# Attention's value products in two passes over a stationary tile that holds both halves of V, with the softmax denominators summed on GpSimd

## The chip, the cores and the metric

The kernel runs on one core of one Trainium2 chip. The metric is the time of one launch in microseconds (us) of device time. The engines are named as the profile names them: PE (TensorE; PEld is its weight load), DVE (VectorE), ACT (ScalarE), POOL (GpSimd) and SP (SyncE, which issues most loads).

## What is computed

The kernel runs two layers of a diffusion trunk for 128 context tokens and 1024 latent tokens, all in fp32. Layer 0 mixes by eight heads of latent attention beside four heads of gated linear attention (GLA), layer 1 is a convolution module, and each layer has a SwiGLU part. The change is in the attention of layer 0:

```
def blocked_attend(q, k, v):
    ...
        s = jnp.einsum('bqhd,bkhd->bhqk', qi, k).astype(jnp.float32) * scale
        p = jax.nn.softmax(s, axis=-1).astype(v.dtype)
        return jnp.einsum('bhqk,bkhd->bqhd', p, v)
```

Context queries see the 128 context keys. Latent queries see 128 cached keys and the 1024 latent ones, so 1152 keys in nine tiles of 128.

## The kernel before

**Products in three passes.** Nearly every matrix product is done on fp32 data split in two: `split` (lines 155 to 157) writes a rounded high part H with an ACT cast and the rest L = x - H with a subtraction on DVE, or on POOL where it is told so. A product A·B is then three matmuls into one PSUM bank: AH·BH, AH·BL and AL·BH.

**Attention.** `att_main(h)` (line 1207) takes a head in three query blocks: 128 context queries against one key tile, and twice 512 latent queries against nine key tiles. For each key tile PE computes the scores transposed (keys on partitions, queries along the row) in three matmuls (lines 1219 to 1221) into one of three banks `ps_s`; ACT takes the exponential (1223) into `p`; the split makes `pH` (ACT) and `pL` (POOL for key tiles 0, 4 and 8, DVE for the others); and three matmuls (1228 to 1230) with `vH` or `vL` as the stationary tile add to the single bank `ps_c`. The stationary `vH` has 128 columns: 64 of V's high part and 64 of ones, set once in `att_head`; in `vL` those 64 are zeros. So the bank holds the output in one half of its partitions and the softmax denominators, 64 times over, in the other half. Two sets of these tiles alternate with the head, and the halves change places with them.

**End of a block.** ACT copies the denominators to `dn` (1235) and computes 1/d as exp(-ln d) (1236, 1237); DVE sharpens it by a Newton step (1238, 1239) and multiplies the output in the bank by it (1241). POOL issues the store to `m_dr` (1251). The bank `ps_c` is free after line 1241.

**What runs beside it.** `braid` (in `layer0_mix`) takes side work at each step of `att_main`: the GLA (`gla_a` beside head 0, `gla_b` beside heads 1 to 6) and `att_prep(h + 1)`, which loads, transposes and splits the next head's q, k and v and finds the row maxima. GLA's large work on the vector engines is lines 906 (every second one on POOL) and 908 (DVE), both products of two SBUF operands.

**What sets the order.** The program's order is not the code's: a scheduler reorders each engine's instructions by its own estimates when the kernel is built, and each engine then works through its list strictly in order, waiting on semaphores.

Of the kernel before, what the change touches and what calls it, by code (L numbers as in the profile page):

```python
# [116 lines left out]
class Trunk:  # L117
# [1009 lines left out]
    def att_setup(self):  # L1127
# [8 lines left out]
        self.qH, self.qL, self.kH, self.kL, self.vH, self.vL = [], [], [], [], [], []  # L1136
# [3 lines left out]
    def att_head(self, ap, i):  # L1140
        nc, NK = self.nc, NT + 1
        one = lambda shape, tag: self.t(ap, shape, f"{tag}{i}", 1, F32R)
        self.qH.append(one([98, NTOK], "qH"))
        self.qL.append(one([QKH, NTOK], "qL"))
        self.kH.append(one([98, NK * P], "kH"))
        self.kL.append(one([QKH, NK * P], "kL"))
        self.vH.append(one([P, NK, P], "vH"))
        self.vL.append(one([P, NK, P], "vL"))
        nc.gpsimd.memset(self.kH[i][96:98, :].bitcast(F32), 1.0)
        d = slice(VH, 2 * VH) if i == 0 else slice(0, VH)  # L1150
        nc.gpsimd.memset(self.vH[i][:, :, d].bitcast(F32), 1.0)
        nc.gpsimd.memset(self.vL[i][:, :, d].bitcast(F32), 0.0)

    def att_prep(self, h):
# [3 lines left out]
        qH, qL, kH, kL, vH, vL = self.qH[i], self.qL[i], self.kH[i], self.kL[i], self.vH[i], self.vL[i]  # L1158
# [17 lines left out]
        vd = slice(i * 64, i * 64 + VH)  # L1176
        self.split(vH[:, :, vd], vL[:, :, vd], vr, nc.gpsimd)
# [28 lines left out]
    def att_main(self, h, mx={}):  # L1206
# [5 lines left out]
        qH, qL, kH, kL, vH, vL = self.qH[i], self.qL[i], self.kH[i], self.kL[i], self.vH[i], self.vL[i]  # L1212
        for q0, N, k0, k1 in ((0, P, 0, 1), (P, 512, 1, NK), (P + 512, 512, 1, NK)):
            acc = self.bank("c")
            qs = slice(q0, q0 + N)
            for kt in range(k0, k1):
# [5 lines left out]
                p = self.t(aq, [P, 512], "p", 4)  # L1222
# [5 lines left out]
                nc.tensor.matmul(acc[:, :N], vH[:, kt, :], pH[:, :N], start=f, stop=False)  # L1228
                nc.tensor.matmul(acc[:, :N], vH[:, kt, :], pL[:, :N], start=False, stop=False)  # L1229
                nc.tensor.matmul(acc[:, :N], vL[:, kt, :], pH[:, :N], start=False, stop=l)  # L1230
                yield
            ns, dd = slice(nb, nb + 64), slice(db, db + 64)
            dn = self.t(aq, [P, 512], "dn", 1)
            rr = self.t(aq, [P, 512], "dr", 2)
            nc.scalar.copy(dn[ns, :N], acc[dd, :N])
            nc.scalar.activation(rr[ns, :N], dn[ns, :N], AF.Ln)
            nc.scalar.activation(rr[ns, :N], rr[ns, :N], AF.Exp, scale=-1.0)
            nc.vector.tensor_mul(dn[ns, :N], dn[ns, :N], rr[ns, :N])
            nc.vector.scalar_tensor_tensor(rr[ns, :N], dn[ns, :N], 2.0, rr[ns, :N],
                                           op0=ALU.subtract, op1=ALU.mult)  # L1240
            nc.vector.scalar_tensor_tensor(rr[ns, :N], acc[ns, :N], -1.0, rr[ns, :N],  # L1241
# [223 lines left out]
```

## Time and profile before

| | |
|---|---|
| median of the runs | 3124.19 us |
| profiled execution: span, first to last instruction | 3122.8 us |
| what lies around the span, by the median | 1.4 us |
| PE busy | 3015.5 us (97%) |
| DVE busy | 2178.5 us (70%) |
| ACT busy | 1232.3 us (39%) |
| POOL busy | 404.6 us (13%) |
| eight heads of attention in the trace | 381 to 898 us |

The profile is of one execution. Its page gives the span; the execution's own time is taken as the span and the 1.4 us around it. Attention takes a sixth of the span, and the engines' shares over the whole kernel say little about it: they are read from that stretch below. Where a stretch has to stand for it, 390 to 895 us is used, 505 us.

### The profile page before, as it was taken

Reading aid. Unit: us, or ns where it says so; the run is one execution under the profiler, and the core shown is the slowest. Engines: PE = TensorE matmul, PEld = TensorE weight load, DVE = VectorE, ACT = ScalarE, POOL = GpSimd, SP = SyncE. Lnnn points to the kernel's source line nnn. Section 1 sums busy time; section 2 is a strip of 40 time slices with the busy share of each in tenths; the row PEclk is TensorE's granted clock in tenths of the full one; section 3 lists DMA queues with packets and bytes.
Section 4 is the critical chain, followed back from the end, with each engine's and each line's share of the span. In section 5 each row is a group of like instructions: output and inputs, shape, how many; then the busy total and the mean of one; then the engine's idle time right before and its main releaser. Section 6 shows DMA issues by size and latency. Waiting matters only on the chain.

```text
span 3122.8 us, 53688 instructions
## 1 busy us (share of the span) xinstructions
PE 3015.5 (97%) x21044; PEld 2819.0 (90%) x21044; DVE 2178.5 (70%) x4110; ACT 1232.3 (39%) x2650; POOL 404.6 (13%) x371
## 2 busy tenths in 40 slices
PE   7999999999989999999999999999999999999999
PEld 5999866766769999999999999999999999999999
DVE  6678468787769889634679996668888875433344
ACT  5323377656654422223422224562222255322222
POOL 1012112112121211111111111111111110000000
PEclk9999989999999999999999999999999999999999
DMA  8545531111164454423232222422222231322222
GB/s 265 168 119 154 151 96 60 51 49 51 37 193 137 128 167 155 141 83 102 79 87 76 82 82 82 141 75 82 84 87 82 82 106 56 110 79 82 81 80 84
DMA packets 449631, 320.46 MB, mean 103 GB/s; under 512 B 29646, under 2 KB 413907, under 8 KB 449378
## 3 DMA queue, kind: packets, MB, share of 16 engines
q1 hardware_dynamic: 411726, 271.06, 28.9%
q0 software_dynamic: 8944, 30.68, 3.1%
q10 hardware_dynamic: 28708, 15.29, 1.8%
q8 instruction: 166, 2.72, 0.4%
q14 instruction: 87, 0.71, 0.1%
HBM read 278.30 MB, written 38.67 MB: 102 GB/s over the span
## 4 chain that ended last, share of the span: by engine, by line
PE 74%; DVE 13%; ACT 6%; DMA 4%; issue 3%; POOL 1%; SPq 0%; ACTq 0%; DVEq 0%; POOLq 0%
PE ps_a L161 12%; PE ps_a L163 12%; PE ps_a L162 12%; PE ps_d L161 6%; PE ps_d L162 6%; PE ps_d L163 6%; PE ps_g L921 2%; DVE ada L292 2%; DVE y L1268 2%; PE ps_a L532 2%; PE ps_a L534 2%; PE ps_a L533 2%; DVE x L409 1%; DVE wL L157 1%; PE ps_c L1229 1%
## 5 line engine op out<-in xcount | busy, mean ns | idle before, releaser
L163 PE MATMUL ps_a<-hH,wL 128*128 128x288 f32 (+2 forms) x3328 | 984.3, 296 | 0.9 <-DVE wL L157 0.9
L162 PE MATMUL ps_a<-hL,wH 128*128 128x288 f32 (+2 forms) x3328 | 984.8, 296 | 0.0
L161 PE MATMUL ps_a<-hH,wH 128*128 128x288 f32 (+2 forms) x3328 | 982.5, 295 | 0.2 <-ACT wH L156 0.2
L156 ACT CAST wH<-wraw 128x1024 fp32r<-128x1024 f32 (+3 forms) x432 | 363.8, 843 | 801.5 <-PE ps_d L162 388.3
L161 PEld LDWEIGHTS ps_a<-hH,wH 128*128 128x128 f32 x3328 | 628.5, 189 | 0.7 <-ACT wH L156 0.5
L163 PEld LDWEIGHTS ps_a<-hH,wL 128*128 128x128 f32 x3328 | 627.3, 189 | 1.5 <-DVE wL L157 1.4
L162 PEld LDWEIGHTS ps_a<-hL,wH 128*128 128x128 f32 x3328 | 627.1, 188 | 0.1
L161 PE MATMUL ps_d<-aH,wH 128*128 128x288 f32 (+2 forms) x1408 | 425.3, 302 | 23.8 <-DVE x L409 13.6
L157 DVE TENSOR_TENSOR wL<-wraw,wH 128x1024 fp32r<-128x1024 f32 (+3 forms) x349 | 338.1, 970 | 130.6 <-ACT wH L156 129.7
L1268 DVE SCALAR_TENSOR_TENSOR y<-u,cvw,y 128x575 f32<-128x575 f32 (+1 forms) x464 | 417.7, 900 | 8.6
L162 PE MATMUL ps_d<-aL,wH 128*128 128x288 f32 (+2 forms) x1408 | 418.2, 297 | 1.4 <-DVE aL L157 1.3
L163 PE MATMUL ps_d<-aH,wL 128*128 128x288 f32 (+2 forms) x1408 | 418.3, 297 | 1.3 <-DVE wL L157 1.3
L409 DVE SCALAR_TENSOR_TENSOR x<-ps_d,par,x 128x288 f32<-128x288 f32 (+3 forms) x520 | 223.4, 452 | 119.7 <-PE ps_d L163 117.1
L161 PEld LDWEIGHTS ps_d<-aH,wH 128*128 128x128 f32 x1408 | 267.8, 190 | 36.9 <-issue 11.4
L157 POOL TENSOR_TENSOR wL<-wraw,wH 128x1024 fp32r<-128x1024 f32 (+2 forms) x83 | 171.9, 2071 | 981.8 <-ACT wH L156 970.8
L162 PEld LDWEIGHTS ps_d<-aL,wH 128*128 128x128 f32 x1408 | 268.1, 190 | 2.7 <-DVE aL L157 2.7
L163 PEld LDWEIGHTS ps_d<-aH,wL 128*128 128x128 f32 x1408 | 268.0, 190 | 1.6 <-DVE wL L157 1.6
L292 DVE SCALAR_TENSOR_TENSOR ada<-ada,scc,ada 128x512 f32<-128x512 f32 (+1 forms) x364 | 230.0, 674 | 20.8 <-DMA ada<-in_w_ada 20.6
L448 DVE TENSOR_TENSOR ev<-ev,ps_a 128x288 f32<-128x288 f32 (+2 forms) x176 | 79.3, 451 | 229.2 <-PE ps_a L163 229.0
L156 ACT CAST aH<-ev 128x288 fp32r<-128x288 f32 (+2 forms) x176 | 75.9, 432 | 330.8 <-DVE ev L448 329.3
L161 PE MATMUL ps_d<-hH,wH 128*128 128x288 f32 (+2 forms) x512 | 153.0, 299 | 10.3 <-DVE dr L1241 6.9
L162 PE MATMUL ps_d<-hL,wH 128*128 128x288 f32 (+2 forms) x512 | 153.1, 299 | 0.1
(331 smaller groups left out, 4901.6 us busy)
## 6 DMA issues: line engine op xcount, KB each, us to landing
wraw<-in_ffn_w_gate SPq DMA_DIRECT2D x88, 512.0 KB
wraw<-in_ffn_w_up SPq DMA_DIRECT2D x88, 512.0 KB
wraw<-in_ffn_w_down SPq DMA_DIRECT2D x144, 256.0 KB
ada<-in_w_ada SPq DMA_DIRECT2D x112, 256.0 KB
wraw<-in_conv_w_pw SPq DMA_DIRECT2D x48, 512.0 KB
in<-in_w_ada SPq DMA_DIRECT2D x8, 1024.0 KB
ada<-in_w_ada SPq DMA_DIRECT2D x64, 128.0 KB
wraw<-in_w_out SPq DMA_DIRECT2D x16, 512.0 KB
```

Source lines behind the costliest of these rows:

```text
L156: self.nc.scalar.copy(H, src)
L157: (eng or self.nc.vector).tensor_sub(L, src, H.bitcast(F32))
L161: mm(out, WH, hH, start=start, stop=False)
L162: mm(out, WH, hL, start=False, stop=False)
L163: mm(out, WL, hH, start=False, stop=stop)
L292: ins = self.nc.vector.scalar_tensor_tensor(acc[v], w, s, acc[v], op0=ALU.mult, op1=ALU.add)
L409: self.nc.vector.scalar_tensor_tensor(X[tt][:, o, s:e], src[:, s:e], gate[:, o, g:g + 1], X[tt][:, o, s:e], op0=ALU.mult, op1=ALU.add)
L448: nc.vector.tensor_mul(pr, sl, bu)
L532: mm(b[:, :wd], hh, wh, start=(k == 0), stop=False)
L533: mm(b[:, :wd], hh, wl, start=False, stop=False)
L534: mm(b[:, :wd], hl, wh, start=False, stop=(k == KD - 1))
L1268: pin(nc.vector.scalar_tensor_tensor(d, u[:, i + o:i + o + w], c, y[:, o:o + w], op0=ALU.mult, op1=ALU.add))
```

## The change

The two tiles `vH` and `vL` become one tile `vHL`: 64 columns of V's high part and, in place of the ones, 64 columns of its low part. Two matmuls a key tile, with `pH` and with `pL` as the moving operand, give vH·p in one half of the bank and vL·p in the other; ACT copies the second half (into a tile under the old tag `dn`) and DVE adds it to the first (`o`). This takes in vL·pL too, which was left out before. The denominators come another way: POOL adds the tiles `p` of a block one by one (`tot`, eight adds to a block of nine key tiles, none to the context block), the sum is split (`tH`, `tL`, in the buffers of `pH` and `pL`; ACT and DVE), and two matmuls with a tile of ones as the stationary operand sum it over the partitions into a bank `ps_s`. Logarithm, exponential and Newton step then read that bank in place of `dn`. `p` has six buffers where it had four. The memsets of ones and zeros go.

```diff
-        self.qH, self.qL, self.kH, self.kL, self.vH, self.vL = [], [], [], [], [], []
+        self.onesR = self.t(ap, [P, P], "onesR", 1, F32R)
+        nc.gpsimd.memset(self.onesR.bitcast(F32), 1.0)
+        self.qH, self.qL, self.kH, self.kL, self.vHL = [], [], [], [], []
...
-        self.vH.append(one([P, NK, P], "vH"))
-        self.vL.append(one([P, NK, P], "vL"))
+        self.vHL.append(one([P, NK, P], "vHL"))
...
-        d = slice(VH, 2 * VH) if i == 0 else slice(0, VH)
-        nc.gpsimd.memset(self.vH[i][:, :, d].bitcast(F32), 1.0)
-        nc.gpsimd.memset(self.vL[i][:, :, d].bitcast(F32), 0.0)
...
-        vd = slice(i * 64, i * 64 + VH)
-        self.split(vH[:, :, vd], vL[:, :, vd], vr, nc.gpsimd)
+        vd, ld = slice(i * 64, i * 64 + VH), slice(64 - i * 64, 128 - i * 64)
+        self.split(vHL[:, :, vd], vHL[:, :, ld], vr, nc.gpsimd)
...
+            tot = None
...
-                p = self.t(aq, [P, 512], "p", 4)
+                p = self.t(aq, [P, 512], "p", 6)
...
-                nc.tensor.matmul(acc[:, :N], vH[:, kt, :], pH[:, :N], start=f, stop=False)
-                nc.tensor.matmul(acc[:, :N], vH[:, kt, :], pL[:, :N], start=False, stop=False)
-                nc.tensor.matmul(acc[:, :N], vL[:, kt, :], pH[:, :N], start=False, stop=l)
+                nc.tensor.matmul(acc[:, :N], vHL[:, kt, :], pH[:, :N], start=f, stop=False)
+                nc.tensor.matmul(acc[:, :N], vHL[:, kt, :], pL[:, :N], start=False, stop=l)
+                if f:
+                    tot = p
+                else:
+                    new = self.t(aq, [P, 512], "tot", 2)
+                    nc.gpsimd.tensor_add(new[:, :N], tot[:, :N], p[:, :N])
+                    tot = new
                 yield
-            ns, dd = slice(nb, nb + 64), slice(db, db + 64)
+            ns, ls = slice(nb, nb + 64), slice(db, db + 64)
+            lo = self.t(aq, [P, 512], "dn", 1)
+            nc.scalar.copy(lo[ns, :N], acc[ls, :N])
+            o = self.t(aq, [P, 512], "o", 1)
+            nc.vector.tensor_add(o[ns, :N], acc[ns, :N], lo[ns, :N])
+            tH = self.t(aq, [P, 512], "pH", 4, F32R)
+            tL = self.t(aq, [P, 512], "pL", 4, F32R)
+            self.split(tH[:, :N], tL[:, :N], tot[:, :N])
+            den = self.bank("s")
+            nc.tensor.matmul(den[:, :N], self.onesR, tH[:, :N], start=True, stop=False)
+            nc.tensor.matmul(den[:, :N], self.onesR, tL[:, :N], start=False, stop=True)
             dn = self.t(aq, [P, 512], "dn", 1)
             rr = self.t(aq, [P, 512], "dr", 2)
-            nc.scalar.copy(dn[ns, :N], acc[dd, :N])
-            nc.scalar.activation(rr[ns, :N], dn[ns, :N], AF.Ln)
+            nc.scalar.activation(rr[ns, :N], den[ns, :N], AF.Ln)
             nc.scalar.activation(rr[ns, :N], rr[ns, :N], AF.Exp, scale=-1.0)
-            nc.vector.tensor_mul(dn[ns, :N], dn[ns, :N], rr[ns, :N])
+            nc.vector.tensor_mul(dn[ns, :N], den[ns, :N], rr[ns, :N])
             nc.vector.scalar_tensor_tensor(rr[ns, :N], dn[ns, :N], 2.0, rr[ns, :N],
                                            op0=ALU.subtract, op1=ALU.mult)
-            nc.vector.scalar_tensor_tensor(rr[ns, :N], acc[ns, :N], -1.0, rr[ns, :N],
+            nc.vector.scalar_tensor_tensor(rr[ns, :N], o[ns, :N], -1.0, rr[ns, :N],
                                            op0=ALU.mult, op1=ALU.mult)
```

Outside attention each engine's order is as before. Three places inside it show what moved; all are at the end of head 3's second long block.

PE before, at the seam between head 3 and head 4: the last value products of head 3 into `ps_c_7380`, and the first scores of head 4 (`ps_s_7685`).

```order
L1228 MATMUL ps_c_7380<-pH_7653,vH_997_4757 128x512
L1229 MATMUL ps_c_7380<-pL_7654,vH_997_4757 128x512
L1230 MATMUL ps_c_7380<-pH_7653,vL_998_4758 128x512
L1219 MATMUL ps_s_7685<-qH_891_4365,kH_893_4367 128x128
L1220 MATMUL ps_s_7685<-qH_891_4365,kL_894_4368 128x128
L1221 MATMUL ps_s_7685<-qL_892_4366,kH_893_4367 128x128
```

PE now, at the same seam (`ps_c_7531` is head 3's bank, `ps_s_7841` the denominators', `ps_s_7853` the first scores of head 4).

```order
L1227 MATMUL ps_c_7531<-pH_7810,vHL_997_4756 128x512
L1228 MATMUL ps_c_7531<-pL_7811,vHL_997_4756 128x512
L1245 MATMUL ps_s_7841<-pH_7837,onesR_4365 128x512
L1246 MATMUL ps_s_7841<-pL_7838,onesR_4365 128x512
L1218 MATMUL ps_s_7853<-qH_892_4367,kH_894_4369 128x128
```

Three value products have become two, and the two ones-matmuls stand between them and the next head's scores.

POOL before, through that block, from the store of the block ahead (`dr_7372`) to its own (`dr_7676`).

```order
L1251 DMA m_dr<-dr_7372 64x512
L157 TENSOR_TENSOR pL_7487<-p_7484,pH_7486 128x512
L906 TENSOR_TENSOR kq_7289<-kq_7289,gqk_7158 128x896
L157 TENSOR_TENSOR pL_7615<-p_7612,pH_7614 128x512
L157 TENSOR_TENSOR vL_998_4758<-vraw_7709,vH_997_4757 128x10x64
L157 TENSOR_TENSOR pL_7692<-p_7689,pH_7691 128x128
L1251 DMA m_dr<-dr_7676 64x512
```

POOL now, from the store of the block ahead (`dr_7524`) to its own (`dr_7845`). Two further adds and line 906 stand just ahead of these rows.

```order
L1264 DMA m_dr<-dr_7524 64x512
L1233 TENSOR_TENSOR tot_7644<-tot_7605,p_7636 128x512
L1233 TENSOR_TENSOR tot_7691<-tot_7644,p_7683 128x512
L1233 TENSOR_TENSOR tot_7719<-tot_7691,p_7711 128x512
L1233 TENSOR_TENSOR tot_7747<-tot_7719,p_7739 128x512
L1233 TENSOR_TENSOR tot_7776<-tot_7747,p_7768 128x512
L157 TENSOR_TENSOR pL_7639<-p_7636,pH_7638 128x512
L1233 TENSOR_TENSOR tot_7816<-tot_7776,p_7808 128x512
L157 TENSOR_TENSOR pL_7771<-p_7768,pH_7770 128x512
L157 TENSOR_TENSOR pL_7860<-p_7857,pH_7859 128x128
L157 TENSOR_TENSOR vHL_997_4756<-vraw_7876,vHL_997_4756 128x10x64
L1264 DMA m_dr<-dr_7845 64x512
```

Eight adds a block stand among POOL's splits, and the split of key tile 4 (`pL_7639`) comes four adds after the add that reads the same `p`.

DVE before, at the end of that block.

```order
L1238 TENSOR_TENSOR dn_7675<-dn_7675,dr_7676 64x512
L952 TENSOR_TENSOR on_7621<-on_7621,sg_7164 128x512
L1239 SCALAR_TENSOR_TENSOR dr_7676<-dn_7675,dr_7676 64x512
L1173 SCALAR_TENSOR_TENSOR kL_996_4756<-ps_p_7711,gaink_norm_4362,kH_995_4755 96x512
L1241 SCALAR_TENSOR_TENSOR dr_7676<-ps_c_7380,dr_7676 64x512
```

DVE now, at the same end.

```order
L157 TENSOR_TENSOR pL_7838<-tot_7816,pH_7837 128x512
L1240 TENSOR_TENSOR o_7835<-ps_c_7531,dn_7833 64x512
L945 TENSOR_SCALAR gss_7749<-gss_7749 128x4
L1251 TENSOR_TENSOR dn_7844<-ps_s_7841,dr_7845 64x512
L176 TENSOR_TENSOR rs_q_1878_7757<-rs_r_1877_7756 128x4
L1252 SCALAR_TENSOR_TENSOR dr_7845<-dn_7844,dr_7845 64x512
L177 TENSOR_TENSOR rs_q_1878_7757<-rs_q_1878_7757,gss_7749 128x4
L1171 SCALAR_TENSOR_TENSOR kL_996_4755<-ps_p_7878,gaink_norm_4362,kH_995_4754 96x512
L178 TENSOR_SCALAR rs_q_1878_7757<-rs_q_1878_7757 128x4
L1254 SCALAR_TENSOR_TENSOR dr_7845<-o_7835,dr_7845 64x512
```

Two operations came ahead of the chain, the split of `tot` and the add that frees the bank; the rest of it is as long as before.

## Rows read from the trace of the kernel before

**Rows 1.** Windows: the attention stretch and three parts of it
```profile
core 0: us, PE busy (x) PEld busy (x) DVE busy (x) ACT busy (x) POOL busy (x), PEclk, DMA share, GB/s
390.00:895.00 505.00, 478.15 (x2476) 343.97 (x2476) 384.90 (x789) 329.77 (x895) 105.52 (x94) 0.94 0.21 63
...
500.00:550.00 50.00, 47.20 (x258) 33.67 (x257) 42.26 (x83) 32.93 (x101) 13.79 (x9) 1.00 0.21 61
550.00:600.00 50.00, 47.88 (x236) 34.14 (x237) 36.11 (x75) 32.11 (x90) 10.34 (x9) 0.86 0.17 49
600.00:650.00 50.00, 48.14 (x263) 34.54 (x262) 42.05 (x89) 27.01 (x78) 6.94 (x5) 1.00 0.15 44
```
**Rows 2.** Chain that ended last, 390 to 895 us, share by line
```profile
by line: PE ps_g L921 13.0%; issue 6.1%; PE ps_c L1229 5.6%; PE ps_c L1228 4.8%; PE ps_c L1230 4.6%; PE ps_p L1191 4.3%; DVE kq L908 3.9%; ACT kq L904 3.3%; PE ps_s L1219 3.3%; DVE pL L157 3.2%; PE ps_s L1220 3.2%; PE ps_s L1221 3.2%; DVE m
```
**Rows 3.** Timeline, PE: successive value products (start us, duration us)
```profile
562.22 0.39 PE L1230 MATMUL ps_c<-pH,vL 128*128 128x512 f32 x1
...
562.45 0.40 PE L1228 MATMUL ps_c<-pH,vH 128*128 128x512 f32 x1
```
**Rows 4.** The tile pH: count, duration ns min/median/max
```profile
L156 ACT CAST pH<-p x152: 284/620/662, 382.0 to 893.4; 128x512 fp32r<-128x512 f32 x144, 128x128 fp32r<-128x128 f32 x8
...
L157 DVE TENSOR_TENSOR pL<-p,pH x112: 673/681/2085, 386.6 to 894.0; 128x512 fp32r<-128x512 f32 x112
L157 POOL TENSOR_TENSOR pL<-p,pH x40: 448/1282/2399, 382.3 to 891.9; 128x512 fp32r<-128x512 f32 x32, 128x128 fp32r<-128x128 f32 x8
```
**Rows 5.** The tiles dn and dr: the block's end, as in rows 4
```profile
L1235 ACT COPY dn<-ps_c x24: 257/577/585, 385.0 to 895.5; 64x512 f32<-64x512 f32 x16, 64x128 f32<-64x128 f32 x8
L1236 ACT ACTIVATE dr<-dn x24: 296/620/634, 385.8 to 896.9; 64x512 f32<-64x512 f32 x16, 64x128 f32<-64x128 f32 x8
L1237 ACT ACTIVATE dr<-dr x24: 297/626/633, 387.0 to 897.6; 64x512 f32<-64x512 f32 x16, 64x128 f32<-64x128 f32 x8
L1238 DVE TENSOR_TENSOR dn<-dn,dr x24: 275/682/690, 387.8 to 898.2; 64x512 f32<-64x512 f32 x16, 64x128 f32<-64x128 f32 x8
L1239 DVE SCALAR_TENSOR_TENSOR dr<-dn,dr x24: 274/680/1075, 388.4 to 899.0; 64x512 f32<-64x512 f32 x16, 64x128 f32<-64x128 f32 x8
L1241 DVE SCALAR_TENSOR_TENSOR dr<-ps_c,dr x24: 273/673/695, 389.3 to 901.5; 64x512 f32<-64x512 f32 x16, 64x128 f32<-64x128 f32 x8
```
**Rows 6.** Waits of PE, 390 to 895 us: us in total, times, longest
```profile
PE ps_s L1219 <- ACT p L1223: 2.5, 2, 1.9
...
PE ps_c L1228 <- DVE dr L1241: 0.5, 1, 0.5
```
**Rows 7.** Groups on DVE, 390 to 895 us: busy us, mean ns
```profile
L157 DVE TENSOR_TENSOR pL<-p,pH 128x512 fp32r<-128x512 f32 x111 | 84.2, 765 | 16.4 <-ACT pH L156 16.0
L908 DVE TENSOR_TENSOR kq<-kq,gqk 128x1152 f32<-128x1152 f32 x18 | 37.7, 2095 | 0.0
```
**Rows 8.** Groups on POOL, 390 to 895 us: busy us, mean ns
```profile
L157 POOL TENSOR_TENSOR pL<-p,pH 128x512 fp32r<-128x512 f32 x32 | 47.0, 1467 | 148.6 <-ACT pH L156 113.1 <-PE ps_p L1191 31.6 <-PE ps_s L1221 3.9
L906 POOL TENSOR_TENSOR kq<-kq,gqk 128x896 f32<-128x896 f32 x9 | 21.0, 2337 | 19.5 <-ACT kq L904 18.4 <-PE ps_p L1191 1.0
...
L157 POOL TENSOR_TENSOR vL<-vraw,vH 128x640 fp32r<-128x640 f32 x6 | 10.1, 1691 | 39.6 <-ACT vH L156 32.9 <-DVE pt L926 6.3 <-ACT kq L904 0.4
...
L157 POOL TENSOR_TENSOR pL<-p,pH 128x128 fp32r<-128x128 f32 x7 | 3.9, 562 | 30.9 <-ACT pH L156 30.9
```
**Rows 9.** Timeline, DVE and POOL at one meeting
```profile
422.31 1.89 DVE L157 TENSOR_TENSOR laL<-zl,laH 128x512 fp32r<-128x512 f32 x1
422.34 1.31 POOL L157 TENSOR_TENSOR pL<-p,pH 128x512 fp32r<-128x512 f32 x1
424.13 0.68 DVE L157 TENSOR_TENSOR pL<-p,pH 128x512 fp32r<-128x512 f32 x1
```

More of the change, by code (lines that the diff above doesn't have):

```diff
@@ L1157, in att_prep @@
         i = h % 2
-        qH, qL, kH, kL, vH, vL = self.qH[i], self.qL[i], self.kH[i], self.kL[i], self.vH[i], self.vL[i]
+        qH, qL, kH, kL, vHL = self.qH[i], self.qL[i], self.kH[i], self.kL[i], self.vHL[i]
         qr = self.t(ap, [P, NT, QKH], "qraw", 1)
@@ L1211, in att_main @@
         nb, db = i * 64, 64 - i * 64
-        qH, qL, kH, kL, vH, vL = self.qH[i], self.qL[i], self.kH[i], self.kL[i], self.vH[i], self.vL[i]
+        qH, qL, kH, kL, vHL = self.qH[i], self.qL[i], self.kH[i], self.kL[i], self.vHL[i]
         for q0, N, k0, k1 in ((0, P, 0, 1), (P, 512, 1, NK), (P + 512, 512, 1, NK)):
```

## The prediction

> **What bounds the kernel now.** I read the page's shares first and set them aside: PE is busy 97% of the whole, but the change lives in a sixth of it. So the windows over the attention stretch come next [rows 1]. There PE's records cover 478 of 505 us, and DVE is busy 385 us, 76%, against 70% in the kernel as a whole; ACT 330; POOL 106, its DMA issues among them. A PE record is longer than what the matmul costs, though: two value products of 512 columns start 0.23 us apart and are recorded with 0.39 and 0.40 us [rows 3]. The price of a matmul is the 0.23, and PE is less full than its busy time says. The chain of waits over the stretch [rows 2] says who holds the end: many short pieces, most of them PE's, the three value products with 5.6, 4.8 and 4.6%, but DVE's with L908 (3.9%) and pL (3.2%) among them. So this is a stage of two engines that are both some three quarters full, each working through its own fixed order. The fullest of the windows shown has DVE at 42.26 of 50 us, 84.5%; I take that as what DVE gets to here.
>
> **The change part by part.**
>
> *PE.* 152 value products go, 144 of 512 columns and 8 of 128 (the casts have the same counts [rows 4]), and 48 ones-matmuls come, 32 and 16. That is 112 long ones fewer and 8 short ones more. At the full distance of 0.23 us: -25.8 us, and at most 8 x 0.23 = +1.8 back, so -24 us. By what the chain gives them it is less: the three lines have 15.0% of 505 us, 75.8 us for some 432 long ones, 0.175 us each, and 112 of these are -19.7 us. I take **-19**, and keep -24 as the end.
>
> *The bank of the value products.* It is free now after six operations, 0.58 + 0.62 + 0.63 + 0.68 + 0.68 + 0.67 = 3.86 us [rows 5]; after the change after the copy and one add, 0.58 + 0.67 = 1.25 us. 2.6 us in 16 long blocks would be -42 us if PE stood and waited each time. It hardly does: its first value product waited for L1241 once, 0.5 us [rows 6], since the scheduler puts scores and GLA in between. I take 0, that row being the nearest, and let the range reach down for the rest. On the other side the denominators now hold one of the three score banks through logarithm, exponential and product, some 0.62 + 0.63 + 0.68 = 1.9 us; 16 times that is +31 us if scores always wanted it, but the scores' wait for ACT at that place is 2.5 us in all [rows 6]. Again 0.
>
> *ACT.* The copy stays. A cast of `tot` comes, 16 x 0.62 and 8 x 0.28 us [rows 4], +12 us on an engine with 175 us idle: hidden. If that cover went it would delay the next exponentials by as much.
>
> *DVE's own work.* Two operations come a block: the add `o` (nearest row L1241, 0.67 and 0.27) and the split of `tot` (0.68 [rows 4], and 0.27 for the short one). 2 x (16 x 0.68 + 8 x 0.27) = **+26 us** on 385.
>
> *POOL, and what it does to DVE.* 8 adds in 16 blocks are 128 operations of the form of POOL's pL, two SBUF operands of 128x512 in and one out: 1.28 us [rows 4], 164 us. POOL's computing is now 47.0 + 21.0 + 10.1 + 3.9 = 82 us [rows 8], 16% of the stretch; it becomes 246 us, 49%. There is room for that on POOL. But the two engines don't run freely beside each other. At 422.31 a DVE subtraction of two SBUF tiles meets a POOL one and takes 1.89 us; the next, alone, takes 0.68 [rows 9]: it ended 0.55 us after POOL did, so it stood still while POOL worked. Over the stretch the pL on DVE have a median of 0.681 and a maximum of 2.085 us [rows 4], a mean of 0.765 [rows 7]: 0.084 us lost in each with POOL at work 16% of the time. POOL pays too: its pL take 1.467 in the mean against a median of 1.282 [rows 4, 8].
>
> The Trainium skill ("SBUF — State Buffer", section "Who interferes with whom") gives this as a rule: a DVE instruction with two SBUF inputs contends with a GpSimd instruction that reads SBUF, and the loser is blocked for the whole of the other; with at most one SBUF input it isn't. The trace agrees with the first half by the 1.89 us of rows 9. By the second half the add `o` and the first Newton product, each with one operand in PSUM, would be free of it. Were they not, 48 more operations at the 0.25 us found below would add 12 us.
>
> With POOL at work 49/16 = 3 times as long, the loss is 0.084 x 3 = 0.25 us for each such operation on DVE. The large groups of them are 112 pL, 18 L908 and 48 of L1238 and L1239 [rows 4, 5, 7], 178; now 24 leave (the first Newton product reads the bank), 48 come (split of `tot`, last product), 202. Without L908, which already meets POOL's half of the same work by its place in the order (mean 2.095 us): 184 x 0.25 - 160 x 0.084 = +33 us. The smaller groups are left out, and exponentials come in bursts, which puts the adds and the splits of the same tiles side by side. I take **+45 us**. The ends are 0 and 128 x 1.28 = 164 us, every add stood out in full by one DVE operation.
>
> *Queues.* The store to `m_dr` stands in POOL's order five adds before the split of key tile 4 (the POOL rows of the change). A late Newton step thus holds adds and a split that PE needs. In PE's order the next head's scores stand behind the two ones-matmuls, and these behind the last add, a cast and a subtraction: 1.28 + 0.62 + 0.68 = 2.6 us, +41 us over 16 long blocks if nothing covered it. The cover is the run of GLA and value products between the last scores of a block and its ones-matmuls. I take 0 and keep the 41 for the upper end.
>
> *Sum.* DVE: 385 + 26 + 45 = 456 us of work and standing still, 90% of 505. By the chain, DVE's pL have 3.2% of 505, 16 us, of 84 us busy, so a fifth of what DVE gains counts: 71 x 0.19 = +13, and with PE's -19 the stage is 6 us shorter. By DVE's ceiling, 456/0.845 = 540 us, it is 35 us longer. As 90% lies above the fullest window I hold the second for nearer, and take +20 us: 505 becomes 525. The profiled execution, 3122.8 + 1.4 = 3124.2 us, equals the median of the runs; **3124.2 + 20 = 3144 us**.
>
> **The rivals.**
>
> *PE stays the bound.* The adds fall into DVE's gaps and the matmuls saved are saved. For it: PE leads the chain [rows 2], and POOL's longest idle times are waits for ACT [rows 8], so adds start at once and are over when DVE comes to its split. Against it: DVE's 76% before anything is added. It gives the full -24: 3124 - 24 = 3100 us; with a few us for the earlier bank, 3092.
>
> *What PE saves is waited away.* PE gives up 19 us and stands that much longer for the GLA chain (L921, 13.0% of the chain, is PE and DVE in turns) and for DVE; the change does its sum but moves nothing. 3124 us, give or take 8.
>
> *The lock decides.* If exponentials come closer together than an add and a split take one after the other (1.28 + 0.68 = 1.96 us), the two engines take turns, and half the 128 adds, say, are stood out in full: +82 us instead of +45. DVE then has 385 + 26 + 82 = 493 us, and at 0.845 the stage takes 583 us: +78, 3202 us. It decides from the point where DVE's standing still passes some +45 and no GLA work is left that PE can do meanwhile. For it: L908 at 2.095 us shows what a regular meeting costs. Against it: pL on DVE start late as a rule, after a queue, so most meetings are chance. A lower granted clock would add to it: 0.94 over the stretch, but 0.86 where PE waited more (550 to 600 us) [rows 1]; 0.08 x 505 = 40 us of which PE's half counts, +20.
>
> **How the numbers follow.** Forecast (DVE becomes the bound, 3144): 0.36. PE stays the bound (3100): 0.26. Nothing moves (3124): 0.22. The lock decides (3202): 0.16. The range of 8 in 10 runs from 3092, the first rival with the bank, to 3205, just past the last. A measurement tells about 2% from no change, 62 us: 3062 and 3187. Faster than that would take more than twice all that PE saves: 0.02. Slower takes the last rival, nearly whole: 0.14. Within: 0.84.
>
> **What would show it.** Right, if the mean of DVE's pL rises from 0.765 to about 0.95 us, DVE is busy 85% or more of attention, the chain there has more of DVE, and the stage is 10 to 50 us longer with all behind it as long as before. The PE part is right if matmuls of ps_c and the ones still start 0.23 us apart and their number falls by 104. The bank's part is wrong if PE waited for it unseen: then the stage is shorter though DVE stands still. The forecast is wrong if pL keeps its 0.77 us with POOL at some 250 us of computing (the adds don't collide), or if the stage gets shorter by 20 us or more.

## The result, and the profile after

| | before | after |
|---|---|---|
| median of the runs | 3124.18 us | 3234.53 us (3230.71 to 3253.57) |
| ratio, 95% interval | | 1.0373 [1.0353, 1.0394] |
| profiled execution: span | 3122.8 us | 3231.2 us |
| attention, first score matmul to the last store to `m_dr` | 380.0 to 902.5, 522.5 us | 381.8 to 1000.0, 618.2 us |
| all behind it | 2220.3 us | 2231.2 us |
| attention: time at the lower level of the granted clock (1.2 GHz) | 65 us | 231 us |
| attention: DVE busy | 396 us | 478 us |
| attention: POOL computing | 84 us | 274 us |

Slower by 110 us by the medians, 116 us by the ratio, and outside the range. One of the four executions of the kernel before took 3606.55 us; the ratio leaves it out. Of the 108 us between the two spans, attention holds 96. The times at 1.2 GHz, here and below, are summed from the trace's records of the granted clock; the windows give them to two digits: 2 x (1 - 0.81) x 610 = 232 us of the stretch below, against 2 x (1 - 0.94) x 505 = 61 us in [rows 1].

Windows over the attention stretch of after, and one part of it (columns as in [rows 1]):

```profile
390.00:1000.00 610.00, 530.44 (x2393) 367.35 (x2392) 474.39 (x846) 347.79 (x928) 292.20 (x218) 0.81 0.16 47
...
640.00:680.00 40.00, 33.42 (x165) 22.48 (x163) 35.98 (x67) 26.31 (x74) 24.63 (x18) 1.00 0.12 37
```

DVE has more to do, but it is busy 474 of 610 us, 78%, no fuller than the 76% before. It isn't at a ceiling: the second row has it at 36 of 40 us, 90%, above the 84.5% that I took for its limit. What changed most in this row is PEclk, 0.94 to 0.81.

The chain that ended last, share by line (beside [rows 2]):

```profile
by line: PE ps_g L921 10.2%; issue 8.7%; DVE pL L157 5.9%; PE ps_c L1228 5.2%; PE ps_p L1189 3.7%; PE ps_s L1218 3.5%; PE ps_s L1220 3.4%; DVE kq L908 3.3%; PE ps_s L1219 3.2%; PE ps_c L1227 3.2%; DVE mx L1190 3.1%; ACT kq L904 2.8%; POOL t
```

It is still many short pieces, with DVE's pL up from 3.2 to 5.9%. PE's waits in that stretch (beside [rows 6]):

```profile
PE ps_c L1228 <- DVE pL L157: 15.8, 18, 3.0
PE ps_c L1228 <- POOL pL L157: 13.7, 16, 2.2
PE ps_p L1189 <- DVE mx L1190: 9.1, 8, 2.9
```

The second value product now waits 29.5 us for its `pL`. Before, the same wait (then line 1229) was 5.3 us:

```profile
PE ps_c L1229 <- POOL pL L157: 2.8, 5, 1.0
PE ps_c L1229 <- DVE pL L157: 2.5, 6, 1.0
```

Most of that growth isn't the adds': run 1 below, which has none, shows 22.0 us. What else grew is PE's standing as a whole, the window less PE's busy time: 618.2 - 536.9 = 81 us of attention, before 522.5 - 488.0 = 34. The first value product shows no wait for its bank, the ones-matmuls wait 1.4 us for the cast of `tot`, and the scores 0.3 us for the bank that the denominators hold.

The groups on DVE (beside [rows 7]) and on POOL (beside [rows 8]):

```profile
L157 DVE TENSOR_TENSOR pL<-p,pH 128x512 fp32r<-128x512 f32 x112 | 110.7, 993 | 6.9 <-ACT pH L156 6.6
...
L1254 DVE SCALAR_TENSOR_TENSOR dr<-o,dr 64x512 f32<-64x512 f32 x16 | 14.9, 932 | 0.3
...
L1252 DVE SCALAR_TENSOR_TENSOR dr<-dn,dr 64x512 f32<-64x512 f32 x16 | 12.5, 783 | 0.2
L1240 DVE TENSOR_TENSOR o<-ps_c,dn 64x512 f32<-64x512 f32 x16 | 11.0, 687 | 19.5 <-ACT dn L1238 19.3
L1251 DVE TENSOR_TENSOR dn<-ps_s,dr 64x512 f32<-64x512 f32 x16 | 11.0, 686 | 7.9 <-ACT dr L1250 7.8
```

```profile
L1233 POOL TENSOR_TENSOR tot<-tot,p 128x512 f32<-128x512 f32 x112 | 166.0, 1482 | 93.1 <-ACT p L1222 59.4 <-DVE pL L157 18.3 <-ACT rs_q L171 5.9
L157 POOL TENSOR_TENSOR pL<-p,pH 128x512 fp32r<-128x512 f32 x32 | 48.5, 1517 | 4.6 <-ACT pH L156 2.7 <-ACT osq L944 1.3 <-PE ps_p L1189 0.6
...
L1233 POOL TENSOR_TENSOR tot<-p,p 128x512 f32<-128x512 f32 x16 | 20.6, 1290 | 84.0 <-ACT p L1222 74.4 <-DVE dn L1251 9.5
```

DVE operations on two SBUF tiles became slower (pL 0.765 to 0.993 us; L1252 and L1254 stand at 0.78 and 0.93). Those with one operand in PSUM, `o` and the first Newton product, kept their 0.69; only 4 of these 32 overlapped an add, but in run 3 below 7 of the 16 last products of a block did, with one operand in PSUM too, and took 0.685 us in the mean. Of the 112 pL, the 43 that overlapped no operation of POOL took 0.683 us in the mean, the 51 that met an add (their longest overlap on POOL) 1.237. The tile views add the spread: pL on DVE has a median of 0.692 and a maximum of 3.467 us (before 0.681 and 2.085 [rows 4]).

The timeline of after shows both ways in which an add costs, and the distance of two ones-matmuls:

```profile
398.45 1.29 POOL L1233 TENSOR_TENSOR tot<-tot,p 128x512 f32<-128x512 f32 x1 [1.58 <-ACT p L1222]
399.71 1.26 POOL L157 TENSOR_TENSOR pL<-p,pH 128x512 fp32r<-128x512 f32 x1
...
401.02 0.50 PE L1228 MATMUL ps_c<-pL,vHL 128*128 128x512 f32 x1 [1.28 <-POOL pL L157]
...
401.51 1.86 DVE L157 TENSOR_TENSOR pL<-p,pH 128x512 fp32r<-128x512 f32 x1
401.51 4.36 POOL L1233 TENSOR_TENSOR tot<-tot,p 128x512 f32<-128x512 f32 x3
...
488.84 0.40 PE L1245 MATMUL ps_s<-pH,onesR 128*128 128x512 f32 x1
489.08 0.40 PE L1246 MATMUL ps_s<-pL,onesR 128*128 128x512 f32 x1
```

First the queue: POOL's split starts when the add ahead of it ends, and PE stands 1.28 us for it. Then the meeting, as in [rows 9]: a pL on DVE beside an add takes 1.86 us. The ones-matmuls are 0.24 us apart, as the value products are in [rows 3].

### The profile page after: what moved, and what is told of

Read it like the earlier page. It is cut to its first block, busy times and chain, and to the rows that moved or that the text cites. A ratio compares the mean times of both kernels' runs of the same rounds, so it can differ in the third digit from the quotient of the medians.

```text
span 3231.2 us, 53804 instructions
## 1 busy us (share of the span) xinstructions
PE 3067.9 (95%) x20940; PEld 2841.6 (88%) x20940; DVE 2262.1 (70%) x4158; ACT 1245.5 (39%) x2674; POOL 592.0 (18%) x496
## 4 chain that ended last, share of the span: by engine, by line
PE 72%; DVE 13%; ACT 5%; issue 4%; DMA 4%; POOL 1%; SPq 0%; ACTq 0%; DVEq 0%; POOLq 0%
PE ps_a L161 12%; PE ps_a L163 12%; PE ps_a L162 12%; PE ps_d L161 6%; PE ps_d L162 6%; PE ps_d L163 6%; PE ps_g L921 2%; DVE ada L292 2%; DVE y L1281 2%; PE ps_a L532 1%; PE ps_a L534 1%; PE ps_a L533 1%; DVE pL L157 1%; DVE x L409 1%; DVE wL L157 1%
## 5 line engine op out<-in xcount | busy, mean ns | idle before, releaser
L1233 POOL TENSOR_TENSOR tot<-tot,p 128x512 f32<-128x512 f32 x112 | 166.0, 1482 | 93.1 <-ACT p L1222 59.4
```

What stands on the lines that cost most here:

```text
L1233: nc.gpsimd.tensor_add(new[:, :N], tot[:, :N], p[:, :N])
```

## The experiments

Twelve kernels ran, in three groups, each group with the kernel before on the same chip (medians 3119.05, 3121.50 and 3118.03 us). Attention and the time at 1.2 GHz are those of the profiled execution. pL is the mean on DVE in ns; in the rows with a star its group also holds splits of other tiles or more of `p`.

| run | median us | ratio to before, 95% | attention us | at 1.2 GHz us | pL |
|---|---|---|---|---|---|
| before | | | 522.5 | 65 | 765 |
| after | 3234.53 | 1.0373 [1.0353, 1.0394] | 618.2 | 231 | 993 |
| 1 after, no adds | 3158.02 | 1.0117 [1.0084, 1.0150] | 544.8 | 135 | 787* |
| 2 after, adds on DVE | 3243.83 | 1.0396 [1.0371, 1.0421] | 628.7 | 243 | 755 |
| 3 before, with adds | 3182.79 | 1.0193 [1.0144, 1.0242] | 573.0 | 99 | 944 |
| 4 after, POOL only writes | 3188.28 | 1.0215 [1.0185, 1.0246] | 562.3 | 172 | 766* |
| 5 run 1, third product | 3164.58 | 1.0150 [1.0120, 1.0179] | 555.0 | 87 | 731* |
| 6 before, two products | 3155.42 | 1.0120 [1.0091, 1.0148] | 554.6 | 172 | 784 |
| 7 after, other ones tile | 3230.86 | 1.0364 [1.0337, 1.0391] | 638.0 | 276 | 1002 |
| 8 after, splits on DVE | 3264.23 | 1.0460 [1.0434, 1.0485] | 654.4 | 313 | 887* |
| 9 before, same lists, third product short | 3140.02 | 1.0063 [1.0047, 1.0080] | 538.0 | 134 | 794 |
| 10 after, same lists, adds short | 3175.88 | 1.0173 [1.0145, 1.0201] | 567.8 | 179 | 786 |
| 11 before, four products | 3145.00 | 1.0081 [1.0065, 1.0097] | 556.1 | 58 | 765 |
| 12 after, three products | 3259.21 | 1.0438 [1.0410, 1.0466] | 651.7 | 212 | 1031 |

### The adds: runs 1 to 4

Run 1, no adds:

```diff
-                else:
-                    new = self.t(aq, [P, 512], "tot", 2)
-                    nc.gpsimd.tensor_add(new[:, :N], tot[:, :N], p[:, :N])
-                    tot = new
...
-            nc.scalar.activation(rr[ns, :N], den[ns, :N], AF.Ln)
+            nc.scalar.activation(rr[ns, :N], den[ns, :N], AF.Ln, bias=1.0)
```

> The changed kernel without the 128 additions on GpSimd (the denominators are those of the first key tile alone, plus 1 under the logarithm). Theory A, the additions and DVE's two-input operations shut each other out: attention falls from 618 us to about 500 and the time to about 3110 us, with the mean of DVE's pL back at 0.77 us and 60 to 80 us of low clock. Theory B, the additions fill GpSimd's queue ahead of its own splits: the same time, 3110 us. Theory C, the new end of a block (split of the sum, ones-matmuls, a score bank held): it stays above 3190 us.

Run 2, the adds on DVE:

```diff
-                    nc.gpsimd.tensor_add(new[:, :N], tot[:, :N], p[:, :N])
+                    nc.vector.tensor_add(new[:, :N], tot[:, :N], p[:, :N])
```

> The changed kernel with the 128 additions on DVE in place of GpSimd. DVE gains 128 x 0.68 = 87 us of its own work, and GpSimd's operations are back at some 82 us. Theory A: about 3150 us, since 63 us of standing still and 87 of work nearly cancel, with pL at 0.77 us mean. Theory B: below 3130 us, for the queue on GpSimd is short again and DVE had room. Theory C: above 3190 us.

Run 3, the kernel before, its value products untouched, with adds for the heads 0 to 6:

```diff
+                if f:
+                    tot = p
+                elif h < HEADS - 1:
+                    new = self.t(self.gp, [P, 512], "tot", 2)
+                    nc.gpsimd.tensor_add(new[:, :N], tot[:, :N], p[:, :N])
+                    tot = new
```

> The kernel before with the same additions on GpSimd in heads 0 to 6 (112 of them), their sums read by nobody; value products and the end of a block are as before. Theories A and B: the additions alone make most of the loss, 3124 + 0.875 x (110 + 15) = about 3225 us. Theory C: 3124 to 3140 us.

Run 4, two writes to `p` in the place of each add (and the bias of run 1):

```diff
-                    new = self.t(aq, [P, 512], "tot", 2)
-                    nc.gpsimd.tensor_add(new[:, :N], tot[:, :N], p[:, :N])
-                    tot = new
+                    nc.gpsimd.memset(p[:, :N], 1.0)
+                    nc.gpsimd.memset(p[:, :N], 1.0)
```

> The changed kernel in which each addition is two memsets of the tile p after its readers are done: GpSimd is held about 2 x 0.52 us each time but reads nothing (the denominators are those of the first key tile alone, plus 1 under the logarithm). Theory A: the time falls to about 3120 us, since an operation that only writes does not meet DVE's second input, and DVE's pL are back at 0.77 us mean. Theory B: it stays above 3190 us, for the queue is as long as with additions. Theory C: above 3190 us.

By the ratios the adds cost 3.73 - 1.17 = 2.56%, 80 us, in the changed kernel, and 1.93%, 60 us, in the kernel before, where 112 of them are all that was added. Run 3 raises pL to 944 ns with nothing added on DVE, run 4 doesn't, with the groups of POOL and DVE reading:

```profile
L1232 POOL MEMSET p<- 128x512 f32 x128 | 65.9, 525 | 114.9 <-DVE pL L157 84.8 <-DVE mneg L1192 20.6 <-DVE mhl L1195 2.7
L1233 POOL MEMSET p<- 128x512 f32 x128 | 65.7, 525 | 3.7
```

```profile
L157 DVE TENSOR_TENSOR pL<-p,pH 128x512 fp32r<-128x512 f32 x128 | 97.0, 766 | 17.8 <-ACT pH L156 15.0 <-PE ps_c L1228 2.2
```

POOL computes 213 us there, and pL keeps its 766 ns; the 40 pL that met a write take 0.686 us in the mean. It is POOL's reads that hold DVE up. Run 2 swaps this meeting for work of DVE's own. On DVE the adds meet only POOL's few operations, pL is back at 755 ns:

```profile
L157 DVE TENSOR_TENSOR pL<-p,pH 128x512 fp32r<-128x512 f32 x112 | 84.5, 755 | 7.1 <-ACT pH L156 6.9
```

but the adds are 100 us of DVE's work, more than the 57 us of standing that go (98 to 41 us, counted as in the part on the prediction), and the kernel is no faster, 3243.8 us. DVE is busy 497 of 629 us there, 79%, hardly more than in after. So the adds cost about the same whether DVE stands beside them or works through them, and run 2 doesn't tell the meeting from other causes. Run 4 costs 30 us over run 1 without any meeting, by POOL's queue and by holding `p` longer. With the adds, whatever way they take, PE stands longer: 46 us of attention in run 1, 54 in run 4, 79 in run 2 and 81 in after, and the time at 1.2 GHz goes from 135 us to 172, 243 and 231. The second value product's wait for pL is not where that shows, 22.0 us in run 1 and 22.8 in run 2. Run 1 held the surprise: without adds there is less work for PE than before, 24 us more for DVE (420 us busy against 396), and still 39 us are lost. Runs 1 and 3 both came out between the times that the theories in their expectations give.

### Less work for PE: runs 5 and 6

Run 5, run 1 with a third value product:

```diff
-                nc.tensor.matmul(acc[:, :N], vHL[:, kt, :], pL[:, :N], start=False, stop=l)
+                nc.tensor.matmul(acc[:, :N], vHL[:, kt, :], pL[:, :N], start=False, stop=False)
+                nc.tensor.matmul(acc[:, :N], vHL[:, kt, :], pH[:, :N], start=False, stop=l)
```

> The changed kernel without the additions, as in e1 (3158 us), with a third value product a key tile put back: the first one is issued a second time, which changes the output and gives PE the 152 matmuls that the change took away. Theory D, a PE that has less to do is granted the low clock for longer and gives the saving back: the low clock falls from 135 us of attention to under 90 and the time is no longer than e1's, 3140 to 3160 us. If instead the matmuls saved were a saving: 152 x 0.23 us more, about 3185 us.

Run 6, the kernel before without its third product:

```diff
-                nc.tensor.matmul(acc[:, :N], vH[:, kt, :], pL[:, :N], start=False, stop=False)
-                nc.tensor.matmul(acc[:, :N], vL[:, kt, :], pH[:, :N], start=False, stop=l)
+                nc.tensor.matmul(acc[:, :N], vH[:, kt, :], pL[:, :N], start=False, stop=l)
```

> The kernel before without the third value product (vL with pH is left out of the output), nothing else: the saving on PE alone. If PE's time counts as the prediction had it: 19 to 24 us less, plus the eleven thousandths that the context blocks bring, so about 3098 us. Theory D: 3110 to 3125 us with more low clock than the 65 us of before. Theory C, that the end of a block makes what e1 lost against before, needs the first of these.

Run 6 does nothing but take 152 matmuls away, and is 34 us slower (3155.4 against 3121.5). DVE's work is the same (394 us), PE stands 59 us of attention instead of 34, and the time at 1.2 GHz goes from 65 to 172 us. The theory of the clock (Theory D) had 3110 to 3125 us here, so the loss is larger than it said. Put back in run 5, 152 matmuls cost 1.50 - 1.17 = 0.33%, 10 us, and not the 152 x 0.23 = 35 us of their distance, and the time at 1.2 GHz falls from 135 to 87; the intervals of runs 1 and 5 overlap, but attention says the same with 10.2 us. The direction fits the clock. But the scheduler had put the lists together anew in both, so the order was a rival.

### The same lists: runs 9 and 10

In these two the scheduler orders the unchanged kernel, and the shapes are cut afterwards, so that every engine has the same instructions in the same order with the same waits.

Run 9:

```diff
-                nc.tensor.matmul(acc[:, :N], vL[:, kt, :], pH[:, :N], start=False, stop=l)
+                self.cuts.append(nc.tensor.matmul(acc[:, :N], vL[:, kt, :], pH[:, :N], start=False, stop=l))
...
+    names = {c.ins.name for c in trunk.cuts}
+    short = lambda a: a.__replace__(ap=[list(a.ap[0]), [1, 32]], bass_ap=None)
+    for bb in nc.main_func.blocks:
+        bb.instructions = [y.__replace__(outs=[short(y.outs[0])], ins=[short(y.ins[0]), y.ins[1]])
+                           if y.name in names else y for y in bb.instructions]
```

> The kernel before with every instruction of every engine in its place and with the same waits; only the third value product (L1230, 152 of them) computes 32 columns instead of 512 or 128, so the low part of V is left out of most of the output. At most 0.23 us each, 34 us of PE's work go. Theory of the clock (PE with less to do gets the lower clock for longer and gives the saving back): time at the lower clock in attention rises from 65 us to over 100 us, and the total does not fall, 3115 to 3155 us. Rival, the order (without the third product the lists are put together anew, and those of the kernel before happen to fit better): with the lists kept, the loss of 34 us is gone; low clock near 65 us, total 3088 to 3115 us.

22 us slower than before, with the same lists and less to do; attention 15.5 us longer, all behind it as long as before (2220.2 us). This is what the theory of the clock expected, and the order is ruled out as the cause of these 22 us. The place where it happens can be read, since instruction for instruction the two are the same (lines of run 9 are one higher). Timeline of PE, before, in head 3:

```profile
632.36 0.39 PE L1230 MATMUL ps_c<-pH,vL 128*128 128x512 f32 x1
632.59 0.39 PE L1228 MATMUL ps_c<-pH,vH 128*128 128x512 f32 x1
632.82 0.39 PE L1229 MATMUL ps_c<-pL,vH 128*128 128x512 f32 x1
633.93 1.04 PE L921 MATMUL ps_g<-kq 64*128 64x128 f32 x8 [0.72 <-DVE pt L924]
634.90 0.44 PE L1191 MATMUL ps_p<-kH,qH 96*128 96x384 f32 x1
```

The same instructions in run 9:

```profile
638.28 0.18 PE L1231 MATMUL ps_c<-pH,vL 128*128 128x32 f32 x1
638.30 0.47 PE L1229 MATMUL ps_c<-pH,vH 128*128 128x512 f32 x1
638.69 0.50 PE L1230 MATMUL ps_c<-pL,vH 128*128 128x512 f32 x1
640.29 1.55 PE L922 MATMUL ps_g<-kq 64*128 64x128 f32 x8 [1.10 <-DVE pt L925]
641.77 0.69 PE L1192 MATMUL ps_p<-kH,qH 96*128 96x384 f32 x1
...
651.69 0.77 PE L1229 MATMUL ps_c<-pH,vH 128*128 128x512 f32 x1
652.26 0.63 PE L1230 MATMUL ps_c<-pL,vH 128*128 128x512 f32 x1
```

PE reaches the GLA product sooner and stands 1.10 us for DVE where it stood 0.72. In run 9 the granted clock then falls. Windows there:

```profile
637.00:641.00 4.00, 2.90 (x16) 2.08 (x15) 4.00 (x6) 0.65 (x2) 1.09 (x1) 0.94 0.00 0
641.00:646.00 5.00, 5.00 (x22) 3.36 (x22) 3.15 (x9) 0.23 (x1) 0.00 (x0) 0.50 0.19 52
...
640.00:668.00 28.00, 27.71 (x112) 19.56 (x112) 11.51 (x29) 5.50 (x16) 1.27 (x1) 0.51 0.10 29
```

and in the kernel before:

```profile
630.00:635.00 5.00, 4.28 (x23) 3.05 (x23) 5.00 (x6) 1.50 (x3) 2.33 (x1) 1.00 0.07 13
635.00:640.00 5.00, 4.96 (x33) 3.18 (x33) 4.55 (x12) 1.23 (x3) 1.27 (x1) 1.00 0.12 43
...
640.00:668.00 28.00, 25.41 (x135) 18.96 (x136) 17.91 (x39) 18.21 (x59) 3.10 (x4) 0.94 0.28 88
```

Before kept 1.00 up to 640 us and 0.94 behind it; run 9 went to 0.50 and stayed there for most of 640 to 668 us. At the lower level two value products start 0.57 us apart (651.69, 652.26) instead of 0.23, every other matmul is longer too, and DVE is idle most of the time (11.5 of 28 us), waiting for PE now. PE "busy" 27.71 of 28 us in that row is 112 slow matmuls. Over attention run 9 has 134 - 65 = 69 us more at 1.2 GHz; at half the speed that is up to 34 us of PE's time. The cut saves at most 144 x 0.21 = 30 us (the next product starts 0.02 us behind the short one at 638.28, and 0.23 behind the long one at 632.36), and 144 x 0.155 = 22 us if a long one counts 0.175 us, as in the step for PE. So +4 to +12 us comes out, and attention got 15.5 us longer. The rest is waits: by the windows over attention, before and in run 9 (columns as in [rows 1]), PE stands 522.5 - 488.0 = 34 us and 538.0 - 497.8 = 40 us.

```profile
380.00:902.50 522.50, 488.02 (x2528) 350.91 (x2528) 395.63 (x809) 343.96 (x927) 108.25 (x97) 0.94 0.22 68
...
380.00:918.00 538.00, 497.78 (x2528) 365.74 (x2528) 397.63 (x809) 343.70 (x926) 106.50 (x98) 0.88 0.22 66
```

Run 10 cuts the first seven adds of each block to 32 columns and gives the eighth `p` for both operands (and the bias of run 1):

```diff
+    def edit(y):
+        if y.name not in cut:
+            return y
+        if cut[y.name] == 7:
+            return y.__replace__(ins=[y.ins[1], y.ins[1]])
+        return y.__replace__(outs=[short(y.outs[0])], ins=[short(x) for x in y.ins])
```

> The changed kernel with every instruction of every engine in its place and with the same waits; of the 128 adds on GpSimd 112 work on 32 columns, and the last of each block adds a tile p to itself, so the denominators are not those of the softmax (the logarithm gets a bias of 1). GpSimd's time for them falls by some 140 us. Theory that the adds' duration costs (the lock between the two engines, and GpSimd's queue): the mean of pL on DVE returns to 0.78 us, the total falls to that of the kernel without adds, 3158 us, give or take 12. Rival, the order: the adds in the estimate put the lists of DVE, ACT and PE together badly, and this stays: total above 3205 us.

3175.9 us: of the 2.56% between after and run 1, 3.73 - 1.73 = 2.00% go with the adds' duration alone, 62 us. Theory and rival both missed their numbers, the theory by 6 us and the rival by 29; the other 0.56% lie in the order, in what the adds still take (POOL computes 149 us instead of 274), or both. pL is back at 786 ns, and the second product's waits for pL fall from 29.5 to 15.7 us (22.0 in run 1, whose lists are others):

```profile
PE ps_c L1229 <- POOL pL L158: 11.1, 16, 1.8
...
PE ps_c L1229 <- DVE pL L158: 4.6, 8, 1.8
```

### More work for PE: runs 11 and 12

Run 11, before with the third product twice:

```diff
-                nc.tensor.matmul(acc[:, :N], vL[:, kt, :], pH[:, :N], start=False, stop=l)
+                nc.tensor.matmul(acc[:, :N], vL[:, kt, :], pH[:, :N], start=False, stop=False)
+                nc.tensor.matmul(acc[:, :N], vL[:, kt, :], pH[:, :N], start=False, stop=l)
```

> The kernel before with the third value product done twice (152 matmuls more, so the low part of V counts twice). At 0.23 us each PE gets 34 us of work more at full clock. Theory of the clock: the time at the lower clock falls below 65 us and takes back a part, total 3110 to 3140 us. Rival, PE is the bound and the clock follows something else: 3150 us or more, low clock 65 us or more. Rival, the order: any new order costs some 30 us on top, 3180 us.

Run 12, after with the first product twice; the edit is that of run 5.

> The changed kernel with a third value product again (the first one done twice, so its part counts twice; 152 matmuls more, 34 us of PE's work at full clock). Theory of the clock: the time at the lower clock in attention falls from 231 us to some 160 us, and the total stays or falls, 3205 to 3245 us. Rival, what waits is DVE and the adds, the clock only follows: the work comes into gaps, total 3234 us with the low clock unchanged at 230 us. Rival, PE is the bound: 3234 + 34 = 3268 us.

Both miss what the theory of the clock expected of them, and are nearer to the rival by which PE is the bound (3150 us or more, and 3268). Run 11 pays 27 us for 152 matmuls, attention 33.6 us; of the 65 us at 1.2 GHz 58 remain. The part behind attention, where the run changes nothing, took 2205.9 us there instead of 2220.3; why isn't known. Run 12 pays 0.65%, 20 us, attention 33.5 us, and 212 us at 1.2 GHz remain of 231. So work added is paid, less what the clock gives back. Counted as 35 us less half of the time at 1.2 GHz that went, run 5 should pay 35 - 24 = 11 us (attention 10.2), run 11 35 - 4 = 31 (33.6) and run 12 35 - 10 = 25 (33.5). How much comes back differs from list to list, and why run 5 got 48 us back and run 12 only 19 stays open.

### The ones tile and the splits: runs 7 and 8

Run 7:

```diff
-        self.onesR = self.t(ap, [P, P], "onesR", 1, F32R)
-        nc.gpsimd.memset(self.onesR.bitcast(F32), 1.0)
+        self.onesR = self.ones.bitcast(F32R)
```

> The changed kernel with the tile of ones for the denominators taken from the constants in place of the attention's memory. In the traces of the changed kernel and of e1 and e4 the eight loads of x for the output projection start at the end of attention, after the last ones-matmul, and the rest of the kernel is 11 us longer; in those of before and e3 they start some 40 us ahead of the end. Theory X, x lies over the tile of ones and waits for its last reader: the loads start some 35 us ahead of the end again, the rest falls from 2231 to 2220 us, and the time is about 3224 us. If not X: 3234 us and 2231 us.

All behind attention takes 2223.2 us instead of 2231.2. In after the loads of `x` for the next stage wait for the last ones-matmul, whose tile lies where `x` goes (the tile view of `x`: 994.1 us, after the last ones-matmul's start at 993.2; before 859.9 us, and run 7 at 958.7 us, 60 us ahead of attention's end):

```profile
L501 POOL DMA_DIRECT2D x<-x_dr x8: 707/717/735, 994.1 to 1003.8; - x8
```

The total, 3230.9 us, can't be told from after's, since attention differed by more than that.

Run 8:

```diff
-                self.split(pH[:, :N], pL[:, :N], p[:, :N], nc.gpsimd if kt % 4 == 0 else nc.vector)
+                self.split(pH[:, :N], pL[:, :N], p[:, :N], nc.vector)
```

> The changed kernel with all splits of p on DVE, so that GpSimd has the additions but nothing that PE waits for. Theory B, the additions make GpSimd's splits late: PE's and PEld's waits for GpSimd's pL (33 us) go and the time falls to about 3210 us although DVE gets 32 x 0.68 = 22 us more. Theory A, the meetings at the port: 3235 to 3260 us, for DVE has more operations that meet the additions.

With all splits on DVE none stands behind an add in POOL's queue, and it is some 30 us slower than after: POOL's queue is not the bottleneck by itself; moved to DVE the same work delays PE as much and more. Nothing that ran beats the kernel before.

## Why the prediction was wrong

**PE's -19 (the step "PE" of the sum) failed, and with the wrong sign.** The count and the distance were right (ones-matmuls 0.24 us apart, 104 matmuls fewer). That the time saved stays saved was not: run 9 takes the third product's columns away in place and loses 22 us, run 6 takes the product itself and loses 34. In run 9 PE stands 6 us longer, and 69 us more of attention are at 1.2 GHz.

**The conversion "by DVE's ceiling", +35, failed.** DVE never came to a ceiling: 78% of attention in after, 79% with the adds on it, 90% in a single window. The line of reasoning that gave +20 rested on it. Run 1 and the change measure its two halves. Without the adds the sum has PE's -19 and DVE's +26, so attention 14 us shorter by the chain and 505 - 411/0.845 = 19 us shorter by the ceiling; in run 1 it is 544.8 - 522.5 = 22 us longer. The adds then move the sum by 8 us by the chain and by 53 by the ceiling; from run 1 to after attention grows by 73.

**The clock stood in the prediction only as an addition of 20 us to the last rival.** It went from 0.94 to 0.81. As arithmetic: attention less half of its time at 1.2 GHz is 522.5 - 32 = 490 us before, 618.2 - 115 = 503 after, 544.8 - 68 = 477 in run 1 and 538.0 - 67 = 471 in run 9. By that measure run 9 gains 19 us, and the change costs +13; that this lies near the forecast's +20, which was chosen between -6 and +35, is luck. All the rest, 83 of 96 us, is time at the lower level. It is an upper bound on the clock's share, since PE also stands in part of that time. The executions on record give a lower price: of one kernel the longer ones have the lower clock. Run 10 took 3157.86 us at a granted clock of 0.973 and 3184.34 at 0.960, 26 us more for 84 us more at 1.2 GHz; a line through each kernel's own executions, 85 in all, gives 0.36 us for each us, as an estimate. By that, 60 of the 96 us are the clock's. Run 9's saving of 22 to 30 us and its 69 us at 1.2 GHz would come to between -5 and +3 us, and with the 6 of PE's standing part of its 15.5 would still be open. And the clock is not the first cause in the chain: run 10 shows that 62 of the change's 116 us (3.73%) go when the adds get short.

The Trainium skill ("TensorE: Matmul & The Clock Gate", section "HAM oscillation — how this bites in real kernels") prices time at the lower level the same way, at half of it. The 0.36 between executions is less, and goes before it. By the half and the counts given with them runs 5 and 11 agree to within 3 us, run 12 to within 8 and run 9 to within 4 to 12; run 6, with 35 us of work less and 107 more at 1.2 GHz, comes to +19, and attention took 32 us more.

**DVE's own work, +26, held**: run 1, which has all of it and no adds, has DVE busy 24 us longer than before.

**POOL and DVE, +45, was somewhat small.** Adds took 166.0 + 20.6 = 187 us, not 164. Taking the lower quartile of each group on DVE (one line, tile and shape) as its price, what lies above it is 98 us in after and 35 before, so +62, inside the ends 0 and 164. pL's mean, 0.95 forecast, is 0.993. That operations with one operand in PSUM stay free held, 0.687 and 0.686 us.

The second half of the rule in the Trainium skill ("SBUF — State Buffer", section "Who interferes with whom") thus holds in this trace, and also what it says of a GpSimd instruction that only writes, by run 4's 766 ns.

**The bank, the score bank and ACT, 0 each, held** as far as the waits show. **Queues, 0,** may have been low. PE's wait for POOL's pL rose by 11 us, but it rose by 8 in run 1 (10.6 us), which has no adds in the queue; what speaks for a price is run 4's 30 us without a meeting. **The rest** is 11 us longer, not "as long as before"; run 7 gives 8 of them to the loads of `x`.

**The rivals.** "The lock decides" (3202) had the right side; its mechanism is there, but in run 2 DVE's own work in its place costs as much. Its +20 for the clock rested on a misreading of [rows 1]: in the window at 0.86 PE's records leave 2.1 us of 50 free, in the one ahead of it, at 1.00, 2.8. "What PE saves is waited away" had the saving lost, but by waits alone: in run 9 these are 6 us. "PE stays the bound" counted PE's saving in full, which run 9 contradicts.

**Open.** What separates run 6 (34 us) from run 9 (22 us), order or the 32 columns left, wasn't tried. How the adds' 80 us divide between POOL's queue and the meeting isn't settled: run 4 puts the first at about 30, but with 132 us of writes for 187 of adds, and with `p` held longer than the adds hold it. Which of PE's waits bring the clock down was seen at one place and not counted, and whether the standing or PE's smaller work does it can't be told, since in runs 6 and 9 both change.

## What to carry to other kernels

Before work is taken off TensorE in a stage where it works hand in hand with another engine, read the granted clock and PE's waits there. Here PE already waited for DVE now and then; with less work on PE those waits grew by 6 us, the clock fell for 69 us more, and more than the saving was lost. Shares of busy time don't show it, since a slow PE looks fuller. To tell this from a changed order, cut shapes in place and keep the lists.

## What the runs showed of the hardware

Removing 480 of 512 columns in 144 matmuls, and 96 of 128 in 8, with no other change made attention 15.5 us longer and the kernel 22 us slower (run 9), with 69 us more at 1.2 GHz. One stand of 1.10 us instead of 0.72 stood ahead of a fall after which the granted clock was 0.51 for 28 us. Twice 128 writes by GpSimd, 132 us, left DVE's two-operand subtractions at 766 ns; 128 adds, 187 us, which read as well, brought them to 993. Beside a write such a subtraction took 0.686 us in the mean (40 of them), beside an add 1.237 (51).
